# Weight rows in 2 KB packets and an fp32 down product in the expert stage of a hybrid decoder block

## The chip, the cores and the metric

The kernel runs on one core of a Trainium2 chip. The metric is the device time of one execution in microseconds (us), lower is better; the median of several runs is given, with the smallest and the largest.

## What is computed

One decoder block over N = 1024 tokens of width D = 1024, all in float32. Stick-breaking attention and a short gated convolution run side by side, are merged by sigmoid gates and projected back. Then comes the part that the change touches, a mixture of experts over 32 experts in 4 groups:

```
x  = x + merged @ w_out
h2 = rms_norm(x, norm_ffn_g)                      # (1024, 1024)
group  = top-1 of h2 @ w_rg + b_rg                # 4 groups
expert = top-2 of h2 @ w_re + b_re inside it      # 8 experts per group
for each expert e:                                # w_gate, w_up: (1024, 256); w_down: (256, 1024)
    act = silu(h @ w_gate[e]) * (h @ w_up[e]) * combine[e]
    y  += act @ w_down[e]
x  = x + y
```

Every expert's weights, 3 MB, are read once: 96 MB in all.

## The kernel before, in words

Attention, convolution, merge and their projections take the first 720 us; an `Order` class sets their order, and the change leaves them as they are. From 720 to 845 us the output projection runs over eight tiles of 128 tokens. For each tile `add_x` makes the new x in one of three buffers XR, `norm2` the norm's factor (on POOL for tiles 0 to 6, on VectorE for tile 7), `put_x` (L866) multiplies x by the norm's gain into HX and has SyncE's queue store it to the scratch tensor `h2d` and x itself to `out`, by column halves; `tr_x` and `route` compute the router's logits, and `rank` and `table` build for every expert a list `idx` of up to 88 token rows (SLOTS). The last two tiles go by column halves, in an order written out by hand.

From 845 us on the expert stage runs. For expert e, `gather` (L1093) fetches its rows from `h2d` by an indirect DMA on POOL's queue; `xT` transposes them on TensorE and splits them into a high and a low fp32r part (ScalarE's copy, VectorE's subtraction); `gateup` multiplies them with the weights in four chunks; `aT` (L1163) transposes the gated activation, `down` multiplies it with two chunks of the down weights, and ScalarE's copy (L1174) and an indirect DMA on POOL's queue that adds into `out` (L1178, the scatter) end the expert. The down product of expert e - 1 stands behind gate and up of expert e. The scatters write one tensor, so each waits until the one before has landed.

A weight chunk is [128, 1024] fp32, 512 KB. `load_chunk` (L799) loads it on SyncE's queue: a gate and up chunk holds rows i*256 + k*128 + p on partition p, so that each piece of a row that is contiguous in both places is 256 floats, 1 KB; a down chunk's are 4 KB. The chunks lie in a ring of 34 buffers (`CH`, named cha, br, chf, mg, vc, chr, x1t, hx and g after the tensors whose space they take). `split_chunk` turns a chunk into a high part (ScalarE, L1103, into WH) and a low part (VectorE, L1104, into WL), in four such buffers, three chunks ahead of TensorE; once a chunk is split, the load of the chunk 34 places on is issued. Every product with split operands is three fp32r products, `mm3`: high by high, high by low, low by high (all at L124, through `mm`).

The loop that handles experts with more than 88 tokens runs no times on this input.

Of the kernel before, what the change touches and what calls it, by code (L numbers as in the profile page):

```python
# [34 lines left out]
DE = 256  # L35
# [5 lines left out]
class Order:  # L41
    """Puts steps given in a plain sequential order into the order in which to issue them: a step
    comes once what it reads is there and what it overwrites is read, the longest chain first."""

# [54 lines left out]
def tile_hybrid_block(  # L99
# [34 lines left out]
    def warm(n):  # L134
        """Products that nothing reads, to keep the array's clock up where it would idle."""
        for _ in range(n):
            mm(PS[:, 1, :], onesB, onesB[:, None, :].to_broadcast([128, 4, 128]), True, True)

    # ------------------------------------------------------------------ constants
    wp = pool("wp")  # L140
# [60 lines left out]

    # ------------------------------------------------------------------ weights of three column blocks
    WR = {}
# [33 lines left out]

    # ------------------------------------------------------------------ first norm, transposed
    xss = xp.tile([128, 8], F32, name="xss")
# [147 lines left out]
    def unit(n, u):  # L387
# [26 lines left out]
        def scan():  # L414
            P = PT[nP]
            # a first row block's last 128 keys of a diagonal unit are all masked
            if diag:
                V.memset(bass.AP(tensor=P.tensor, offset=P.offset + w - 128, ap=[P.ap[0], [516 + 128, 2], [1, 1]]), 1.0)
            for j in range(2):
                pr = P[:, j, 0:w - 128 if diag and j == 0 else w][:, ::-1]  # L420
                V.tensor_tensor_scan(pr, pr, pr, 1.0 if diag else P[:, j, w:w + 1], op0=OP.mult, op1=OP.bypass)  # L421
            if c:
                V.tensor_copy(PT[(n + 1) % 2][:, :, 512:513], P[:, :, 0:1])
# [10 lines left out]
        for sp in range(w // 256):  # L434
            tr, x = 4 + state["sp"] % 2, state["sp"] % 3
            state["sp"] += 1
            # quarters (key block, row block); the masked one of a diagonal unit is zero
            last = diag and sp == w // 256 - 1
# [141 lines left out]

    # ------------------------------------------------------------------ transposed blocks of the other projections
    hlp = pool("hlp")
# [184 lines left out]

    # ------------------------------------------------------------------ output projection, second norm, routing
    rc = pool("rc", side="right")
# [29 lines left out]
    def load_chunk(r, i, wg, wu, wd, Y=Y):  # L799
        if i < 4:  # L800
            v = r.rearrange("p (k j c) -> p k j c", k=2, j=2)
            for j, w in enumerate((wg, wu)):
                Y.dma_start(v[:, :, j], w[i * 256:(i + 1) * 256].rearrange("(k p) c -> p k c", p=128))
        else:
            Y.dma_start(r, wd[(i - 4) * 128:(i - 3) * 128])

    def load_upto(n, ring=0, Y=Y):
        while lst["n"] < min(n, len(chunks)):
            e, i = chunks[lst["n"]]
            load_chunk(CH[lst["n"] % (ring or len(chunks))], i, w_gate_e[0, e], w_up_e[0, e], w_down_e[0, e], Y)  # L810
            lst["n"] += 1
# [54 lines left out]
    def put_x(t, half):  # L866
        tsl, hs = slice(t * 128, (t + 1) * 128), slice(half * 512, (half + 1) * 512)
        G.tensor_mul(HX[:, hs], XR[t % 3][:, hs], g2[:, hs])  # L868
        Y.dma_start(h2d[tsl, hs], HX[:, hs])
        Y.dma_start(out[tsl, hs], XR[t % 3][:, hs])  # L870
# [16 lines left out]
    def route(t):  # L887
# [26 lines left out]
        st[t] = OH, ohs, tw  # L914
        # combine weights times the norm's factor
        G.tensor_scalar(s[:, 1:2], m8[:, 0, 0:1], -1.0, None, op0=OP.mult)
# [90 lines left out]
    for t in range(2, 6):  # L1007
# [10 lines left out]
        load_upto(NCA + 11 + t - 2)  # L1018
    # the last two tiles by column halves
    for m, (half, t) in enumerate(((0, 6), (0, 7), (1, 6), (1, 7))):  # L1020
# [39 lines left out]
    table(7)  # L1060
    # slot tables
    t2 = sm.tile([128, NE], F32, name="t2")
# [3 lines left out]

    # tiles past the first of each expert, as a running count
    ext = rc.tile([128, NE], F32, name="ext")
# [13 lines left out]

    # ------------------------------------------------------------------ experts
    me = pool("me", side="right")
# [3 lines left out]
    AC = [me.tile([SLOTS, DE], F32, name="ac")] * 2  # L1088
    ACT_ = [me.tile([128, 2, 2, SLOTS], F32R, name="act")] * 2
    gate = dram.tile([1, 16], F32, name="gate")  # L1090
# [5 lines left out]

    split = {chunks[i]: HW[i] for i in range(4)}
    cst2 = {"n": 4, "h": 4}

    def split_chunk(r, key):  # L1100
        wh, wl = HW[cst2["h"] % len(HW)]
        cst2["h"] += 1
        S.activation(wh, r, AF.Copy)  # L1103
        V.tensor_sub(wl, r, wh)  # L1104
        split[key] = (wh, wl)

    def split_upto(n):
        while cst2["n"] < min(n, len(chunks)):
            e, i = chunks[cst2["n"]]
            split_chunk(CH[cst2["n"] % NC], (e, i))  # L1110
            cst2["n"] += 1
            load_upto(cst2["n"] + NC, NC)

    def expert_mm(e, i, xt, at, o):
        wh, wl = split.pop((e, i))
        if i < 4:
            for kk in range(2):
                k = 2 * i + kk
                cs = slice(kk * 512, (kk + 1) * 512)
                mm3(o, xt[0][:, k], xt[1][:, k], wh[:, cs], wl[:, cs], k == 0, k == 7)  # L1120
        else:
            k = i - 4
            for half in range(2):
                hs = slice(half * 512, (half + 1) * 512)
                mm3(PS[0:SLOTS, 2 + half, :], at[:, 0, k], at[:, 1, k], wh[:, hs], wl[:, hs], k == 0, k == 1)

# [13 lines left out]
    def gateup(e):  # L1140
        xt = XET[e % 2]
        o = PS[0:SLOTS, e % 2, :]
        sg, ac = SG[e % 2], AC[e % 2]
        for i in range(4):
            if i == 2 and e:
                aT(e - 1)
            if i == 3 and e + 1 < NE:
                xT(e + 1)
                if e + 3 < NE:
                    gather(e + 3)  # L1150
            expert_mm(e, i, xt, None, o)
            pos["n"] += 1
            if i < 3 or e < NE - 1:
                split_upto(pos["n"] + 3)
        S.activation(sg, o[:, 0:DE], AF.Silu, scale=rsl[0:SLOTS, e:e + 1])
        V.scalar_tensor_tensor(ac, o[:, DE:2 * DE], wsl[0:SLOTS, e:e + 1], sg, op0=OP.mult, op1=OP.mult)
        split_upto(pos["n"] + 3)

    def aT(e):
        ac, at = AC[e % 2], ACT_[e % 2]  # L1160
        pb = PS[:, 6, 0:2 * SLOTS].rearrange("p (k c) -> p k c", c=SLOTS)
        for k in range(2):
            T.transpose(pb[:, k], ac[:, k * 128:(k + 1) * 128], identF[0:SLOTS, 0:SLOTS])  # L1163
        S.activation(at[:, 0], pb, AF.Copy)  # L1164
        V.tensor_sub(at[:, 1], pb, at[:, 0])

    def down(e):
        at, ye = ACT_[e % 2], YE[e % 2]
        for k in range(2):
            expert_mm(e, 4 + k, None, at, None)  # L1170
            pos["n"] += 1
            split_upto(pos["n"] + 3)
        if e < NE - 1:
            S.activation(ye, PS[0:SLOTS, 2:4, :].rearrange("p b c -> p (b c)"), AF.Copy)  # L1174
        else:
            S.activation(ye[:, 0:512], PS[0:SLOTS, 2, :], AF.Copy)
            V.tensor_copy(ye[:, 512:1024], PS[0:SLOTS, 3, :])
        G.indirect_dma_start(out=out[:, :], out_offset=bass.IndirectOffsetOnAxis(ap=idx[0:SLOTS, e:e + 1], axis=0),  # L1178
                             in_=ye[:, :], in_offset=None, compute_op=OP.add)
# [3 lines left out]
    gather(1)  # L1183
    # the loads that follow stay behind the first gathers
    G.tensor_copy(AC[0][0:1, 0:1], g2[0:1, 0:1])
    for i in range(1, 4):
        early_l(i)
    load_upto(NC + 4, NC)
    xT(0)
# [9 lines left out]

    # ------------------------------------------------------------------ tokens past an expert's first slots  # L1200
    lpt = CH[6]
# [10 lines left out]
    with tc.For_i(0, nx, 1):  # L1212
# [25 lines left out]
        xT(0)  # L1238
        for i in range(6):
            split_chunk(CH[i], (-1, i))  # L1240
            expert_mm(-1, i, XET[0], ACT_[0], PS[0:SLOTS, 0, :])
            if i == 3:
                sg, ac = SG[0], AC[0]
                S.activation(sg, PS[0:SLOTS, 0, 0:DE], AF.Silu, scale=wx[0:SLOTS, 2:3])
                V.scalar_tensor_tensor(ac, PS[0:SLOTS, 0, DE:2 * DE], wx[0:SLOTS, 1:2], sg, op0=OP.mult, op1=OP.mult)
                aT(0)
        S.activation(YE[0], PS[0:SLOTS, 2:4, :].rearrange("p b c -> p (b c)"), AF.Copy)
# [32 lines left out]
```

## Time and profile before

| what | value |
|---|---|
| time, median of 3 runs (smallest, largest) | 1202.77 us (1201.70, 1204.35) |
| the profiled execution's span | 1199.3 us (the page gives no other time of its own) |
| TensorE busy | 1114.5 us, 93% |
| VectorE busy | 757.6 us, 63% |
| ScalarE busy | 644.9 us, 54% |
| POOL busy | 363.0 us, 30% |
| q1, SyncE's queue | 140360 packets, 148.12 MB, 38.2% of 16 engines' span |
| q0, POOL's indirect queue | 9216 packets, 19.95 MB, 7.7% |
| mean granted TensorE clock | 0.974 |

The page's second part cuts the span into 40 slices; the expert stage is the last 12 of them. There the DMA engines are busy nine tenths or more in nearly every slice, and hardly before. A share over the whole span therefore says little of the stage that the change touches. Busy time of POOL counts the issue of its indirect transfers; the time that they take is in the queues' rows and in the chain of waits, where a line gives start, length and what ran.

### The profile page before, as it was taken

To read this page: it belongs to the slowest core of one execution; us is meant where nothing else is said; L and a number is where in the kernel's file an instruction comes from. 1 tells how busy PE (TensorE), PEld (TensorE's weight loads), DVE (VectorE), ACT (ScalarE), POOL (GpSimd) and SP (SyncE) were. 2 spreads that over 40 slices of the span, in tenths; PEclk is the share of its full clock that TensorE was granted. 3 is DMA by queue.
4 is the path that set the end of the run, shared out by engine and by line. 5 is a ranking of instruction groups with operands and counts; after the bars stand their busy time and mean duration, and the time that the engine had idled before them with its cause. 6 is when DMAs were issued, how large, how long until landed. Compare 5 with 4: busy or idle time off the path is not lost.

```text
span 1199.3 us, 16771 instructions
## 1 busy us (share of the span) xinstructions
PE 1114.5 (93%) x5761; PEld 893.6 (75%) x5761; DVE 757.6 (63%) x1317; ACT 644.9 (54%) x1204; POOL 363.0 (30%) x658
## 2 busy tenths in 40 slices
PE   6999898999999999999999999998899999899883
PEld 5988897987888888888888887786566656566552
DVE  5579989989885332333324073445598889688772
ACT  6586767777653213222223142223588878687672
POOL 4636466463000000000000004555363334333211
PEclk9999999998999999999999999999899999899897
DMA  6000101011011111111121168928899999999993
GB/s 222 27 27 14 40 2 40 15 29 34 1 36 54 53 36 45 53 53 52 37 62 45 36 189 290 322 73 276 241 316 312 323 323 292 310 314 317 328 322 82
DMA packets 149666, 169.18 MB, mean 141 GB/s; under 512 B 14381, under 2 KB 129097, under 8 KB 149577
## 3 DMA queue, kind: packets, MB, share of 16 engines
q1 hardware_dynamic: 140360, 148.12, 38.2%
q0 software_dynamic: 9216, 19.95, 7.7%
q8 instruction: 46, 0.75, 0.2%
q14 instruction: 44, 0.35, 0.1%
HBM read 150.72 MB, written 20.45 MB: 143 GB/s over the span
## 4 chain that ended last, share of the span: by engine, by line
PE 52%; DMA 27%; DVE 8%; issue 5%; POOL 4%; ACT 2%; SPq 1%; POOLq 0%; DVEq 0%; ACTq 0%
PE PS L124 49%; DMA out_dram<-xr,idx 10%; DMA out_dram<-ye,idx 8%; DVE pt L421 3%; PE PS L446 2%; DMA cha<-in_w_down_e_dram 2%; DMA xr<-h2d,idx 1%; DMA chr<-in_w_up_e_dram 1%; DVE WL L231 1%; DVE ahl L466 1%; POOL hx L868 1%; PE PS L338 1%; DMA chr<-in_w_down_e_dram 1%; DMA mg<-in_w_down_e_dram 1%; DMA h2d<-hx 1%
## 5 line engine op out<-in xcount | busy, mean ns | idle before, releaser
L124 PE MATMUL PS<-hH,WH 128*128 128x512 f32 x448 | 143.9, 394 | 1.1 <-DVE attF L478 1.1
L124 PE MATMUL PS<-hH,WL 128*128 128x512 f32 x448 | 142.0, 390 | 0.0
L124 PE MATMUL PS<-hL,WH 128*128 128x512 f32 x448 | 141.9, 389 | 0.0
L124 PE MATMUL PS<-WH,xet 128*88 128x512 f32 x384 | 137.9, 410 | 3.5 <-ACT WH L1103 3.5
L421 DVE TENSOR_TENSOR_SCAN pt<-pt 128x128 f32<-128x128 f32 (+2 forms) x96 | 92.8, 1008 | 18.5 <-issue 13.4
L674 POOL TENSOR_TENSOR mg<-mg,sga 128x1024 f32<-128x1024 f32 x6 | 14.7, 2456 | 293.0 <-DVE sga L672 293.0
L124 PEld LDWEIGHTS PS<-hH,WL 128*128 128x128 f32 x448 | 84.1, 188 | 17.7
L124 PEld LDWEIGHTS PS<-hH,WH 128*128 128x128 f32 x448 | 84.1, 188 | 17.4 <-ACT WH L610 1.2
L124 PEld LDWEIGHTS PS<-hL,WH 128*128 128x128 f32 x448 | 84.2, 188 | 16.4
L124 PE MATMUL PS<-WH,hH 128*128 128x384 f32 x256 | 91.9, 359 | 4.4 <-ACT hH L268 2.3
L611 DVE SCALAR_TENSOR_TENSOR WL<-br,cols,WH 128x128 fp32r<-128x128 f32 x200 | 68.9, 411 | 29.3 <-ACT WH L610 29.3
L124 PE MATMUL PS<-WH,hL 128*128 128x384 f32 x256 | 87.2, 341 | 0.0
L124 PE MATMUL PS<-WL,hH 128*128 128x384 f32 x256 | 86.8, 339 | 0.0
L615 DVE TENSOR_TENSOR WL<-br,WH 128x512 fp32r<-128x512 f32 x16 | 11.1, 691 | 116.5 <-ACT WH L614 116.5
L610 ACT ACTIVATE WH<-br,cols 128x128 fp32r<-128x128 f32 x200 | 65.4, 392 | 35.6 <-PE PS L124 34.4
L124 PE MATMUL PS<-WL,xet 128*88 128x512 f32 x192 | 79.2, 413 | 4.9 <-DVE WL L1104 4.4
L124 PEld LDWEIGHTS PS<-WH,xet 128*88 128x88 f32 x384 | 61.3, 160 | 29.5 <-ACT WH L1103 4.1
L124 PE MATMUL PS<-WH,act 128*88 128x512 f32 x192 | 65.5, 395 | 1.2 <-ACT act L1164 1.2
L1178 POOL DMA_INDIRECT out_dram<-xr,idx x16 | 35.2, 2200 | 100.7 <-DMA out_dram<-ye,idx 56.0
L460 POOL CAST ahl<-zeros 128x256 fp32r<-128x256 f32 x32 | 30.4, 958 | 115.5 <-PE PS L124 107.0
L124 PE MATMUL PS<-ahl,vt 128*128 128x256 f32 x320 | 53.7, 298 | 11.4 <-DVE attF L478 10.7
L1178 POOL DMA_INDIRECT out_dram<-ye,idx x16 | 31.5, 1970 | 99.6 <-DMA out_dram<-xr,idx 75.7
(278 smaller groups left out, 2726.2 us busy)
## 6 DMA issues: line engine op xcount, KB each, us to landing
br<-in_w_in_dram SPq DMA_DIRECT2D x25, 512.0 KB
cha<-in_w_gate_e_dram SPq DMA_DIRECT2D x42, 256.0 KB
cha<-in_w_up_e_dram SPq DMA_DIRECT2D x42, 256.0 KB
cha<-in_w_down_e_dram SPq DMA_DIRECT2D x18, 512.0 KB
mg<-in_w_down_e_dram SPq DMA_DIRECT2D x17, 512.0 KB
mg<-in_w_gate_e_dram SPq DMA_DIRECT2D x29, 256.0 KB
mg<-in_w_up_e_dram SPq DMA_DIRECT2D x29, 256.0 KB
br<-in_w_in_dram SPq DMA_DIRECT2D x36, 192.0 KB
```

The costliest lines, as they stand in the source:

```text
L124: T.matmul(o, a, b, start=start, stop=stop)
L231: V.scalar_tensor_tensor(WL3[:, k], WR[idx, k // 2][:, k % 2], g1[:, k:k + 1], WH3[:, k], op0=OP.mult, op1=OP.subtract)
L338: T.transpose(pb[:, j].bitcast(F32R), st[:, a, j * 128:(j + 1) * 128], identR)
L421: V.tensor_tensor_scan(pr, pr, pr, 1.0 if diag else P[:, j, w:w + 1], op0=OP.mult, op1=OP.bypass)
L446: T.transpose(PS[:, tr, q * 128:(q + 1) * 128], BT[n % 3][:, j, (sp * 2 + sj) * 128:(sp * 2 + sj + 1) * 128], identF)
L460: G.tensor_copy(AHL[x][:, :, 0:128], zeros[:, None, :].to_broadcast([128, 2, 128]))
L466: V.tensor_sub(AHL[x][:, 1, lo:512], PS[:, tr, lo:512], AHL[x][:, 0, lo:512])
L610: S.activation(j.wH[:, k], r[:, k], AF.Copy, scale=g1[:, k:k + 1])
L611: V.scalar_tensor_tensor(j.wL[:, k], r[:, k], g1[:, k:k + 1], j.wH[:, k], op0=OP.mult, op1=OP.subtract)
L674: (G if b < 6 else V).tensor_add(mg, mg, mst[b].rearrange("p (t c) -> p t c", c=128))
L868: G.tensor_mul(HX[:, hs], XR[t % 3][:, hs], g2[:, hs])
L1178: G.indirect_dma_start(out=out[:, :], out_offset=bass.IndirectOffsetOnAxis(ap=idx[0:SLOTS, e:e + 1], axis=0), in_=ye[:, :], in_offset=None ...
```

## The change

Four things change. Gate and up chunks take their rows as p*8 + k instead of k*128 + p, so two rows lie behind one another in DRAM on each partition and a contiguous piece is 2 KB; the chunk's inside is ordered gate, then up. To match, `put_x` stores the tokens' rows with column p*8 + k at place k*128 + p: it multiplies only once both halves are there, in two POOL instructions that read every eighth element, and stores 512 KB at once. The down weights are no longer split: `down` is four fp32 products (two chunks by two column halves) straight from the loaded chunks, with an activation that isn't split either, so the two ScalarE copies and two VectorE subtractions per expert for the down chunks and VectorE's subtraction in `aT` go. And a load into a chunk's buffer is issued by `took` when that chunk has been read: a gate and up chunk after its split, a down chunk after its products. (Comments were taken out as well.)

```diff
     def load_chunk(r, i, wg, wu, wd, Y=Y):
         if i < 4:
-            v = r.rearrange("p (k j c) -> p k j c", k=2, j=2)
+            v = r.rearrange("p (j k c) -> p j k c", k=2, j=2)
             for j, w in enumerate((wg, wu)):
-                Y.dma_start(v[:, :, j], w[i * 256:(i + 1) * 256].rearrange("(k p) c -> p k c", p=128))
+                Y.dma_start(v[:, j], w.rearrange("(p k) c -> p k c", k=8)[:, 2 * i:2 * i + 2])
...
     def put_x(t, half):
         tsl, hs = slice(t * 128, (t + 1) * 128), slice(half * 512, (half + 1) * 512)
-        G.tensor_mul(HX[:, hs], XR[t % 3][:, hs], g2[:, hs])
-        Y.dma_start(h2d[tsl, hs], HX[:, hs])
+
+        if half:
+            for q in range(2):
+                c = slice(q * 512, (q + 1) * 512)
+                G.tensor_mul(HX.rearrange("t (k p) -> t k p", k=8)[:, :, q * 64:q * 64 + 64],
+                             XR[t % 3][:, c].rearrange("t (p k) -> t k p", k=8), g2[:, c].rearrange("t (p k) -> t k p", k=8))
+            Y.dma_start(h2d[tsl, :], HX)
         Y.dma_start(out[tsl, hs], XR[t % 3][:, hs])
...
-    ACT_ = [me.tile([128, 2, 2, SLOTS], F32R, name="act")] * 2
+    ACT_ = [me.tile([128, 2, SLOTS], F32, name="act")] * 2
...
+    order = [c for c in chunks if c[1] < 4]
+    place = {c: n for n, c in enumerate(chunks)}
+    read = set()
+
+    def took(c):
+
+        read.add(place[c])
+        while lst["n"] < len(chunks) and lst["n"] - NC in read:
+            load_upto(lst["n"] + 1, NC)
...
     def split_upto(n):
-        while cst2["n"] < min(n, len(chunks)):
-            e, i = chunks[cst2["n"]]
-            split_chunk(CH[cst2["n"] % NC], (e, i))
+        while cst2["n"] < min(n, len(order)):
+            c = order[cst2["n"]]
+            split_chunk(CH[place[c] % NC], c)
             cst2["n"] += 1
-            load_upto(cst2["n"] + NC, NC)
...
+            took(c)
...
+    def down_mm(e, k, r):
+        for half in range(2):
+            mm(PS[0:SLOTS, 2 + half, :], ACT_[e % 2][:, k], r[:, half * 512:(half + 1) * 512], k == 0, k == 1)
...
     def aT(e):
-        ac, at = AC[e % 2], ACT_[e % 2]
+        ac = AC[e % 2]
...
-        S.activation(at[:, 0], pb, AF.Copy)
-        V.tensor_sub(at[:, 1], pb, at[:, 0])
+        S.activation(ACT_[e % 2], pb, AF.Copy)
 
     def down(e):
-        at, ye = ACT_[e % 2], YE[e % 2]
+        ye = YE[e % 2]
         for k in range(2):
-            expert_mm(e, 4 + k, None, at, None)
-            pos["n"] += 1
-            split_upto(pos["n"] + 3)
+            down_mm(e, k, CH[place[e, 4 + k] % NC])
+            took((e, 4 + k))
```

Two places show how instructions move. On TensorE, between the transposes of the next expert's rows (identF by xr) and the next expert's gate and up products (WH, WL or hw by xet), before (`act` is the activation of the expert before):

```order
L1134 MATMUL PS<-identF,xr_5949 128x88 x8
L124 MATMUL PS<-hw_7083,xet_7082 88x512 x6
L124 MATMUL PS<-WH,act 88x512
L124 MATMUL PS<-WL,act 88x512
L124 MATMUL PS<-WH,act 88x512 x2
L124 MATMUL PS<-WL,act 88x512
L124 MATMUL PS<-WH,act 88x512 x2
L124 MATMUL PS<-WL,act 88x512
L124 MATMUL PS<-WH,act 88x512 x2
L124 MATMUL PS<-WL,act 88x512
L124 MATMUL PS<-WH,act 88x512
```

The same place after; mg, and in other experts another buffer of the ring, is the loaded chunk itself:

```order
L1146 MATMUL PS<-identF,xr_5950 128x88 x8
L124 MATMUL PS<-hw_7075,xet_7073 88x512 x6
L124 MATMUL PS<-mg,act 88x512 x4
L124 MATMUL PS<-WH,xet_7074 88x512
```

Twelve products became four, at the same place. The second place is POOL's order around the second norm of tile 6 (n2s is where its sum is made; hx from xr_5949 is tile 6, from xr_5950 tile 7; oha and ohb belong to the ranking), before:

```order
L868 TENSOR_TENSOR hx<-xr_5950,g_5954 128x512
L945 TENSOR_TENSOR oha<-oha,ohs 128x32
L946 CAST ohb<-oha 128x32
L868 TENSOR_TENSOR hx<-xr_5949,g_5954 128x512
L874 TENSOR_TENSOR n2s<-n2s 128x1
L190 TENSOR_SCALAR nrM<-n2s 128x1
```

And after:

```order
L950 TENSOR_TENSOR oha<-oha,ohs 128x32
L951 CAST ohb<-oha 128x32
L872 TENSOR_TENSOR hx<-xr_5949,g_5954 128x8x64 x2
L879 TENSOR_TENSOR n2s<-n2s 128x1
L190 TENSOR_SCALAR nrM<-n2s 128x1
```

The multiplies of the first halves of tiles 6 and 7 no longer stand earlier in the program; both of a tile now come together, tile 6's right before its norm, and tile 7's in the same way where its second half's stood, before the routing of that tile.

## Rows read from the trace of the kernel before

**Rows 1.** The page: span and the scatters' groups.

```profile
span 1199.3 us, 16771 instructions
...
L1178 POOL DMA_INDIRECT out_dram<-xr,idx x16 | 35.2, 2200 | 100.7 <-DMA out_dram<-ye,idx 56.0
...
L1178 POOL DMA_INDIRECT out_dram<-ye,idx x16 | 31.5, 1970 | 99.6 <-DMA out_dram<-xr,idx 75.7
```

**Rows 2.** Chain of waits, 930 to 1060 us: start, length, what.

```profile
936.32 8.68 DMA out_dram<-xr,idx
...
945.87 8.61 DMA out_dram<-ye,idx
...
976.81 8.38 DMA out_dram<-xr,idx
...
1028.01 9.83 DMA out_dram<-ye,idx
```

**Rows 3.** POOL timeline, 865 to 1199.3 us: start, length, instruction, [idle before].

```profile
869.52 2.30 POOL L1178 DMA_INDIRECT out_dram<-xr,idx  x1 [4.18 <-ACT xr L1174]
...
976.81 1.59 POOL L1178 DMA_INDIRECT out_dram<-xr,idx  x1 [7.42 <-DMA out_dram<-ye,idx]
...
1012.80 7.09 POOL L1178 DMA_INDIRECT out_dram<-xr,idx  x1 [4.24 <-ACT WH L1103]
...
1161.10 1.57 POOL L1178 DMA_INDIRECT out_dram<-xr,idx  x1 [11.66 <-ACT xr L1174]
...
1185.69 1.57 POOL L1178 DMA_INDIRECT out_dram<-ye,idx  x1 [6.31 <-DMA out_dram<-xr,idx]
```

**Rows 4.** TensorE (PE) timeline, 900 to 912 us.

```profile
900.11 0.32 PE L1163 MATMUL PS<-identF,ac 88*128 88x88 f32 x2
...
903.66 0.40 PE L124 MATMUL PS<-WH,act 128*88 128x512 f32 x1
...
906.47 0.39 PE L124 MATMUL PS<-WH,xet 128*88 128x512 f32 x1
...
909.23 0.32 PE L1163 MATMUL PS<-identF,ac 88*128 88x88 f32 x2
```

**Rows 5.** VectorE (DVE) timeline, 1008.5 to 1020.4 us.

```profile
1012.43 1.22 DVE L1104 TENSOR_TENSOR WL<-g,WH 128x1024 fp32r<-128x1024 f32 x1
...
1015.83 1.22 DVE L1104 TENSOR_TENSOR WL<-cha,WH 128x1024 fp32r<-128x1024 f32 x1
```

**Rows 6.** DMA, 1184 to 1192.2 us: queue, issue with median landing.

```profile
q0 software_dynamic: 144, 0.36, 31.0%
...
out_dram<-ye,idx POOLq DMA_INDIRECT x1, 6.5
```

**Rows 7.** DMA queue, 937.9 to 945.0 us: packets, MB, share.

```profile
q1 hardware_dynamic: 1752, 1.79, 72.9%
```

**Rows 8.** POOL timeline, 819 to 836 us, tile 6.

```profile
821.96 1.29 POOL L868 TENSOR_TENSOR hx<-xr,g 128x512 f32<-128x512 f32 x1 [0.68 <-DVE xr L863]
```

**Rows 9.** TensorE timeline, 825 to 840 us, router.

```profile
832.35 2.21 PE L124 MATMUL PS<-wrt,xr 128*128 128x36 f32 x16
```

**Rows 10.** VectorE groups by shape, 900 to 1160 us.

```profile
L1104 DVE TENSOR_TENSOR WL<-cha,WH 128x1024 fp32r<-128x1024 f32 x37 | 44.5, 1217 | 12.5 <-ACT WH L1103 8.4 <-ACT xr L1174 4.2
...
L1136 DVE TENSOR_TENSOR xet<-PS,xet 128x352 fp32r<-128x352 f32 x50 | 23.8, 517 | 0.1
```

**Rows 11.** DMA queue, 737 to 744 us, 2 KB stores.

```profile
q1 hardware_dynamic: 674, 1.37, 50.6%
```

**Rows 12.** DMA queue, 1029.6 to 1037.8 us.

```profile
q1 hardware_dynamic: 1500, 2.17, 80.3%
```

**Rows 13.** DMA queue, 978.4 to 985.2 us.

```profile
q1 hardware_dynamic: 1061, 1.65, 67.3%
```

**Rows 14.** DMA queues, 870 to 1167 us.

```profile
q1 hardware_dynamic: 59363, 75.79, 77.7%
q0 software_dynamic: 8076, 17.60, 27.1%
```

More of the change, by code (lines that the diff above doesn't have):

```diff
@@ L1107, in split_upto, with gateup_mm @@
     def split_upto(n):
-        while cst2["n"] < min(n, len(chunks)):
-            e, i = chunks[cst2["n"]]
-            split_chunk(CH[cst2["n"] % NC], (e, i))
+        while cst2["n"] < min(n, len(order)):
+            c = order[cst2["n"]]
+            split_chunk(CH[place[c] % NC], c)
             cst2["n"] += 1
-            load_upto(cst2["n"] + NC, NC)
[L1114 to L1125, printed above, removed]
+            took(c)
+    def gateup_mm(e, i, xt, o):
+        wh, wl = [w.rearrange("p (j k c) -> p k j c", k=2, j=2) for w in split.pop((e, i))]
+        o = o.rearrange("p (j c) -> p j c", j=2)
+        for kk in range(2):
+            k = 2 * i + kk
+            mm3(o, xt[0][:, k], xt[1][:, k], wh[:, kk], wl[:, kk], k == 0, k == 7)
+    def down_mm(e, k, r):
+        for half in range(2):
+            mm(PS[0:SLOTS, 2 + half, :], ACT_[e % 2][:, k], r[:, half * 512:(half + 1) * 512], k == 0, k == 1)
     def xT(e):
@@ L1150, in gateup @@
                     gather(e + 3)
-            expert_mm(e, i, xt, None, o)
+            gateup_mm(e, i, xt, o)
             pos["n"] += 1
@@ L1187, in tile_hybrid_block @@
         early_l(i)
-    load_upto(NC + 4, NC)
+    load_upto(NC)
+    for i in range(4):
+        took(chunks[i])
     xT(0)
@@ L1238, in tile_hybrid_block @@
         xT(0)
-        for i in range(6):
+        for i in range(4):
             split_chunk(CH[i], (-1, i))
[L1241 to L1246, printed above, removed]
+            gateup_mm(-1, i, XET[0], PS[0:SLOTS, 0, :])
+        sg, ac = SG[0], AC[0]
+        S.activation(sg, PS[0:SLOTS, 0, 0:DE], AF.Silu, scale=wx[0:SLOTS, 2:3])
+        V.scalar_tensor_tensor(ac, PS[0:SLOTS, 0, DE:2 * DE], wx[0:SLOTS, 1:2], sg, op0=OP.mult, op1=OP.mult)
+        aT(0)
+        for k in range(2):
+            down_mm(0, k, CH[4 + k])
         S.activation(YE[0], PS[0:SLOTS, 2:4, :].rearrange("p b c -> p (b c)"), AF.Copy)
```

## The prediction, made before the changed kernel had run

> **What bounds the kernel now.** I began with the page. TensorE is busy 93% of a span of 1199.3 us, which invites the reading "TensorE bound", but that share is an average, and the change touches only the last 380 us, so I read that stretch alone. The page's groups show it first: the 32 scatters of L1178 take 35.2 + 31.5 us on POOL's queue and POOL stands idle some 100 us ahead of each half of them, mostly for the landing of the other half [rows 1]. Second, the chain of waits over 930 to 1060 us: nearly every microsecond is a scatter in flight. A scatter issued at 936.32 lands 8.68 us later, and the next is issued 0.87 us after that, at 945.87 [rows 2]. They all add into `out`, so each waits for the one before. Third, POOL's timeline: from the scatter at 869.52 to that at 1185.69 lie 31 periods in 316.2 us, **10.20 us per expert** [rows 3]. TensorE needs less: between the transposes of `aT` of two experts lie 909.23 - 900.11 = 9.12 us [rows 4]. So the scatter chain sets the pace, TensorE has 1.1 us per expert to spare, and the last scatter is followed by 13.6 us that don't change.
>
> What makes a scatter slow is to be seen in two places. (a) POOL's issue of one takes 1.57 to 1.59 us when nothing disturbs it, but 7.09 us at 1012.80 [rows 3], and just then VectorE runs one 1.22 us subtraction of L1104 after another without a gap [rows 5]. (b) The landing: in a stretch with an otherwise idle queue it is 6.5 us [rows 6]; beside 1 KB weight packets 8.68 and 8.61 us [rows 2, 7].
>
> The profiled execution's span is 1199.3 us, 3.5 below the median of 1202.77; the page gives no other time of its own. I sum on the span and add 3.5.
>
> **The change, part by part.**
>
> *The head (put_x).* Before tile 6's second norm POOL had one multiply of 1.29 us (821.96) [rows 8], and one like it before tile 7's routing. Now both multiplies of a tile stand there, and they read every eighth element. If a strided one costs what the contiguous one does, that is 2 x 1.29 = 2.6 us more on the path to the first gather; if double, 1.29 x (2 x 2 - 1) x 2 = 7.7 us. The shared buffer HX is free only after a store of 512 KB instead of 256 KB, some tenths. No strided POOL multiply of this size is in the trace. I take **+4.0 us**, near the lower end, since norm and routing also wait for other engines in places. [...] The half multiplies that go from tile 6's and 7's earlier places lie in POOL's idle time: nothing.
>
> *Down product on TensorE.* Twelve products of 0.23 us go (903.66 to 906.47: 2.81 us), four fp32 products come. An fp32 product is two instructions (8 router products are x16 [rows 9]). If each costs as much per column as now, 8 x 0.234 = 1.87 us; if twice that, 16 x 0.234 = 3.74. I take 3.6, near the upper end: three fp32r products now stand for one and leave out low times low, which a full fp32 product cannot, so that four for three is the likely cost. That makes a TensorE period of 9.12 - 2.81 + 3.6 = 9.9 us. Still under 10.2, hence 0 now; but it is the floor if the scatters get faster than 9.9.
>
> *Splits that go.* Per expert VectorE loses two of six subtractions of 1.217 us, and the small one of L1165; two of 0.517 stay: 6 x 1.217 + 2 x 0.517 = 8.34 us of splits before, 5.90 after [rows 10]. A TensorE wait for a split is never last on the scatter chain, so the only gain is in (a). The 32 issues took 66.7 us [rows 1] where 32 x 1.59 = 50.9 would do: 15.8 us of excess. VectorE's load of splits falls to 0.71, and its long gapless strings, which do the harm, should fall by more. I take 0.6 of the excess: **-9.5 us**; ends -3 (gate and up chunks still come in strings) and -14.
>
> *Larger weight packets.* In a window with q1 packets of 1 KB, packet time is 72.9% x 16 engines x 7.1 us / 1752 = 47.3 ns [rows 7]; where only 2 KB packets moved, 50.6% x 16 x 7.0 / 674 = 84 ns [rows 11]. Two thirds of the weight bytes move at 84 instead of 94.6 ns per 2 KB: 11% less queue time. But loads are not what is waited for until late. What counts more: a scatter shares the engines with them. Beside mixed 1 and 4 KB packets, 80.3% x 16 x 8.2 / 1500 = 70 ns on average, a scatter landed in 9.83 us, another in such a mix (67.3% x 16 x 6.8 / 1061 = 69 ns, at 976.81) in 8.38 [rows 2, 12, 13]: 9.1 on average against 8.65 beside 1 KB alone. So 23 ns longer packets go with +0.46 us. With 2 KB packets the 1 KB stretches grow by 37 ns and the mixed ones too. Lower end: nothing, if the share goes by bytes. Upper end: in proportion to the 2.15 us above the idle landing, 2.15 x 37 / 47.3 = +1.7, and 2.3 with the mixed stretches. I take +0.5 us, the measured step, on the 28 scatters before the loads thin out: **+14 us**; ends 0 and +64 (the latter can't stand whole, see the rivals).
>
> *The end.* From 870 to 1167 us q1 takes 77.7% and q0 27.1%: the queues are full [rows 14], and the loads lose their lead. Only once does it reach the scatter chain: at 1161.10 POOL had been idle 11.66 us, against 7.42 us in a steady stretch and 6.31 at the end [rows 3], so 4.2 to 5.4 us; I take 4.6. q1's 0.777 x 297 = 231 us [rows 14], by 11% of some 70% (gate and up), makes the loads end up to 18 us sooner. This stall goes: **-4.6 us**; what is late next is the scatter again, so no more than that. Down chunks are now freed when TensorE has read them and not after their split, some three of 34 chunks less lead: hidden while the loads are ahead; once they are behind, slots stand free and no load waits for one: 0. If that cover failed it would cost a stall like the one above, up to 5 us.
>
> *Sum.* 4.0 - 9.5 + 14 - 4.6 = +3.9; 1199.3 + 3.9 + 3.5 = **1206.7 us**.
>
> **The rivals.**
> - *The landing doesn't care about packet size* (faster). For it: 8.38 us in a mix [rows 2]. Then 4.0 - 9.5 - 4.6 = -10.1; per expert 0.3 us less, 9.9, just where TensorE's floor lies, so it gets no better: about 1193 us. It decides as long as a scatter lands less than 0.2 us later than now.
> - *Landing in proportion to packet size* (much slower). For it: 8.65 at 47 ns, 9.83 at 70 ns is close to proportion. Against: 8.38. A slower chain lets the loads catch up, then the engines fall idle at times, and landings go back toward 6.5; so I halve the +2.1 us that would be left to about +1.0 per scatter: 28 + 4.0 - 9.5 - 4.6 = +17.9, 1221 us. It decides where the mean landing passes 9.6 us.
> [...]
>
> **How the numbers follow.** A measurement of this kernel tells about 0.2% (2.4 us) from no change. Forecast (1206.7) 0.38, of which a little falls below 1205.2; landing unchanged 0.30; in proportion 0.17; cancelled 0.15. Faster 0.32 (the first rival, and a little of the cancelled case with a large relief), same 0.17, slower 0.51. The range goes from 1191 (the fast rival with a head of 2.6) to 1222 (the proportional one); the forecast's own range, by the two ends of the relief, is 1202 to 1213.
>
> **What would show it.** In the profile after: mean issue of a scatter 1.7 to 1.8 us instead of 2.1; mean landing 9.5 to 10 us; period about 10.4; strided multiplies over 1.3 us each and the first gather some 4 us later; TensorE's four down products in 3.5 to 3.7 us; no idle of 11 us before a scatter near the end. Wrong if landings stay at 8.6 to 9 us and the period falls to 9.9 (fast rival), if the down products take far over 3.7 us so that TensorE becomes the pace, or if the chain runs through loads instead of scatters.

## The result and the profile after

The changed kernel takes 1208.13 us (median of 14 runs, 1204.60 to 1213.99) against 1202.44 for the kernel before in the same sessions: a ratio of 1.0054, 95% interval 1.0037 to 1.0071. It is slower by half a per cent. I had written 1206.7. The number is close; how it comes about is not what I wrote, as the runs below show.

The profiled execution after has a span of 1211.3 us, and its time on record is 1213.48 us, so it is one of the slower runs of its kernel, while the one of before stood near its median. The medians differ by 5.7 us, so about half of the 12 us between the two spans is chance. What I read from the pair is therefore checked on the kernels below, which have profiles of their own.

From the page of the changed kernel, the answer to [rows 1], with q1's row:

```profile
span 1211.3 us, 16407 instructions
...
q1 hardware_dynamic: 106440, 148.12, 37.1%
...
L1188 POOL DMA_INDIRECT out_dram<-xr,idx x16 | 27.7, 1730 | 108.3 <-DMA out_dram<-ye,idx 53.6
...
L1188 POOL DMA_INDIRECT out_dram<-ye,idx x16 | 26.8, 1675 | 104.6 <-DMA out_dram<-xr,idx 66.9
```

The scatters' issue fell from 66.7 to 54.5 us, by 12.2, as the step on the splits foresaw. q1 moves the same bytes in 106440 packets instead of 140360.

POOL's timeline after, from 815 us on, the answer to [rows 8] and [rows 3]:

```profile
825.15 2.01 POOL L872 TENSOR_TENSOR hx<-xr,g 128x512 f32<-128x512 f32 x1
...
831.49 2.02 POOL L872 TENSOR_TENSOR hx<-xr,g 128x512 f32<-128x512 f32 x1 [4.33 <-DVE xr L863]
...
841.64 4.15 POOL L872 TENSOR_TENSOR hx<-xr,g 128x512 f32<-128x512 f32 x2
...
857.68 1.31 POOL L1098 DMA_INDIRECT xr<-h2d,idx  x1 [0.85 <-issue]
...
884.01 1.63 POOL L1188 DMA_INDIRECT out_dram<-xr,idx  x1 [3.81 <-ACT xr L1184]
...
1197.80 1.57 POOL L1188 DMA_INDIRECT out_dram<-ye,idx  x1 [5.59 <-DMA out_dram<-xr,idx]
```

And the first gather of the kernel before, on the same view:

```profile
844.86 1.31 POOL L1093 DMA_INDIRECT xr<-h2d,idx  x1 [0.92 <-issue]
```

A strided multiply takes 2.01 us, not 1.29; the first gather comes 12.8 us later in this pair, not 4. (Two kernels below with the same `put_x`, e3 and e4, have it at 848.15 and 850.46 us, the ones with contiguous multiplies between 840.1 and 846.8.) From first to last scatter lie 1197.80 - 884.01 = 313.8 us, 10.12 per expert instead of 10.20: the stage behind the head is hardly faster, though its scatters are issued 12 us faster. And the stall near the end, which was to go, is still there on the same view:

```profile
1170.66 1.57 POOL L1188 DMA_INDIRECT out_dram<-xr,idx  x1 [10.30 <-ACT xr L1184]
1181.08 1.57 POOL L1188 DMA_INDIRECT out_dram<-ye,idx  x1 [8.85 <-DMA out_dram<-xr,idx]
```

TensorE's timeline after, one expert, the answer to [rows 4]:

```profile
904.83 0.32 PE L1175 MATMUL PS<-identF,ac 88*128 88x88 f32 x2
...
908.38 3.60 PE L124 MATMUL PS<-chr,act 128*88 128x512 f32 x8
...
914.59 0.32 PE L1175 MATMUL PS<-identF,ac 88*128 88x88 f32 x2
```

Four products in eight instructions, which take 3.60 us by this row, and a period of 9.76 us, by which the down product costs 9.76 - 9.12 + 2.81 = 3.45 us. I had put in 3.6.

The DMA view over 297 us of the stage after (885 to 1182 us), to be held against [rows 14], with the scatters' median landing in us:

```profile
q1 hardware_dynamic: 35288, 77.65, 76.1%
q0 software_dynamic: 8064, 17.55, 26.8%
...
out_dram<-xr,idx POOLq DMA_INDIRECT x15, 9.4
out_dram<-ye,idx POOLq DMA_INDIRECT x15, 9.2
```

The same landings before (870 to 1167 us):

```profile
out_dram<-xr,idx POOLq DMA_INDIRECT x15, 9.3
out_dram<-ye,idx POOLq DMA_INDIRECT x14, 8.5
```

Scatters land a little later, and the weights move 77.65 instead of 75.79 MB in an equally long window: 2.5% more, far from 11%. Before, 1000 bytes take 0.777 x 16 x 297 us / 75.79 MB = 48.7 ns of an engine, after 46.6. The 84 ns of a 2 KB packet that I had taken [rows 11] were those of a store with nothing beside it.

The end of the chain of waits after, from 1105 us on, shows what I had not looked for:

```profile
1116.69 13.05 DMA chr<-in_w_up_e_dram
...
1129.76 11.07 DMA x1t<-in_w_up_e_dram
...
1140.85 11.46 DMA cha<-in_w_up_e_dram
...
1162.97 9.29 DMA chf<-in_w_down_e_dram
...
1172.33 9.67 DMA mg<-in_w_up_e_dram
...
1190.65 6.29 DMA out_dram<-xr,idx
```

And the same place before, where the loads stand too, though the stretch that I had read ended ahead of them:

```profile
1141.83 10.46 DMA cha<-in_w_down_e_dram
...
1152.30 7.77 DMA br<-in_w_up_e_dram
...
1160.09 6.93 DMA mg<-in_w_up_e_dram
```

The last load in the chain lands at 1182.00 after and 1167.02 before, 29 and 32 us ahead of the span's end. So I formed theory L: **the weight loads set the end**. By it they run from the moment at which the first experts free buffers until the last chunk is there, on engines that are full all the while (q1 76.1% and q0 26.8% of them in the window above), and the head delays that moment.

### The profile page after: what moved, and what is told of

Read it like the earlier page. It is cut to its first block, busy times and chain, and to the rows that moved or that the text cites. A ratio compares the mean times of both kernels' runs of the same rounds, so it can differ in the third digit from the quotient of the medians.

```text
span 1211.3 us, 16407 instructions
## 1 busy us (share of the span) xinstructions
PE 1133.4 (94%) x5633; PEld 878.8 (73%) x5633; DVE 687.2 (57%) x1221; ACT 586.4 (48%) x1140; POOL 358.2 (30%) x658
## 3 DMA queue, kind: packets, MB, share of 16 engines
q1 hardware_dynamic: 106440, 148.12, 37.1%
## 4 chain that ended last, share of the span: by engine, by line
PE 59%; DMA 20%; DVE 8%; POOL 5%; issue 4%; ACT 2%; SPq 0%; POOLq 0%; DVEq 0%; ACTq 0%
PE PS L124 56%; DMA out_dram<-xr,idx 6%; DMA out_dram<-ye,idx 5%; DVE pt L421 3%; PE PS L446 2%; DVE ahl L466 1%; DMA chr<-in_w_up_e_dram 1%; DMA chr<-in_w_gate_e_dram 1%; DVE WL L231 1%; POOL hx L872 1%; DMA cha<-in_w_up_e_dram 1%; DMA x1t<-in_w_up_e_dram 1%; DMA mg<-in_w_up_e_dram 1%; DMA x<-in_x_dram 1%; DMA chf<-in_w_down_e_dram 1%
## 5 line engine op out<-in xcount | busy, mean ns | idle before, releaser
L124 PE MATMUL PS<-WH,xet 128*88 128x512 f32 x384 | 143.5, 433 | 0.0
L124 PE MATMUL PS<-WL,xet 128*88 128x512 f32 x192 | 76.5, 398 | 0.0
L124 PE MATMUL PS<-ahl,vt 128*128 128x256 f32 x320 | 54.5, 301 | 11.1 <-DVE attF L478 10.3
L1188 POOL DMA_INDIRECT out_dram<-xr,idx x16 | 27.7, 1730 | 108.3 <-DMA out_dram<-ye,idx 53.6
L1188 POOL DMA_INDIRECT out_dram<-ye,idx x16 | 26.8, 1675 | 104.6 <-DMA out_dram<-xr,idx 66.9
L405 ACT ACTIVATE pt<-PS 128x1024 f32<-128x1024 f32 (+1 forms) x48 | 42.5, 885 | 30.8 <-PE PS L124 30.2
```

What stands on the lines that cost most here:

```text
L124: T.matmul(o, a, b, start=start, stop=stop)
L405: S.activation(PT[nP][:, :, 0:w], z, AF.Sigmoid, scale=-1.0)
```

## The experiments

Each line is timed against the kernel before on the same chip. Ratios are to the kernel before, with their 95% interval. Lines of different chips stand in the table (the kernel before has 1202.28 to 1204.69 us on them), so lines are better compared by their ratios than by their medians; the two can differ by a few us.

| kernel | median us | ratio | interval |
|---|---|---|---|
| the change | 1208.13 | 1.0054 | 1.0037 to 1.0071 |
| e1, permutation in xT instead of put_x | 1199.39 | 0.9981 | 0.9965 to 0.9996 |
| e2, fp32 down alone | 1202.64 | 1.0002 | 0.9983 to 1.0020 |
| e3, 2 KB packets and put_x alone | 1206.92 | 1.0041 | 1.0026 to 1.0056 |
| e4, the change with 1 KB packets | 1216.29 | 1.0111 | 1.0096 to 1.0127 |
| e5, the change with contiguous multiplies | 1200.27 | 0.9995 | 0.9977 to 1.0013 |
| e6, before, scatters into two tensors | 1202.81 | 1.0014 | 0.9993 to 1.0034 |
| e7, before, last three experts' loads left out | 1198.50 | 0.9955 | 0.9935 to 0.9976 |
| e8, e1 with 1 KB packets | 1205.09 | 1.0030 | 1.0002 to 1.0059 |
| e9, e6 and e7 together | 1201.63 | 0.9997 | 0.9984 to 1.0010 |
| e10, e1 with a ring of 36 chunks | 1206.66 | 1.0045 | 1.0028 to 1.0062 |
| e11, e1 with the split down product | 1198.31 | 0.9950 | 0.9932 to 0.9968 |
| e12, e6 with 28 loads left out, spread | 1179.10 | 0.9783 | 0.9764 to 0.9801 |

### The parts one by one: e1 to e4

e1 leaves `put_x` as it was and permutes in `xT`:

```diff
-            T.transpose(pb[:, k], xe[:, kk * 128:(kk + 1) * 128], ...)
+            T.transpose(pb[:, k], xe.rearrange("t (p k) -> t k p", k=8)[:, kk], ...)
```

> The change with put_x as it was before (two contiguous multiplies, two stores, no permutation) and the permutation made in xT instead: each transpose takes every eighth column of the gathered rows. Everything after the head stays as in the changed kernel. In the profiles the first gather of the changed kernel is issued at 857.68 us, that of the kernel before at 844.86. Theory H (the head is the cost, and it is three times what I put into the sum): the first gather comes back to about 845, and the time falls by some 12 us to about 1196, below the kernel before. Theory P (my prediction: larger packets make the scatters land later, the head is worth 4): only some 4 us come back, 1204. If the strided transposes cost TensorE time, its period per expert rises above the 9.76 us of the changed kernel.

1199.39 us, 8.7 less than the change; its first gather is issued at 840.13. Theory H holds, with somewhat less than the 12 us of the one profile. The strided transposes are not free. TensorE's timeline of e1, from one expert to the next:

```profile
942.02 1.02 PE L1141 MATMUL PS<-identF,xr 88*128 88x88 f32 x8
...
952.02 1.02 PE L1141 MATMUL PS<-identF,xr 88*128 88x88 f32 x8
```

And of the change:

```profile
945.41 0.77 PE L1146 MATMUL PS<-identF,xr 88*128 88x88 f32 x8
...
955.17 0.77 PE L1146 MATMUL PS<-identF,xr 88*128 88x88 f32 x8
```

The period is 10.00 us in e1 instead of 9.76. Its scatters come every 9.98 us from first to last, so there TensorE itself is about as slow as what it feeds.

e2 takes the changed kernel with `load_chunk`, `put_x` and the order inside a chunk as before.

> Only the fp32 down product (with the loads issued as chunks are read); gate and up rows in 1 KB packets and put_x as before. Theory P: only the relief of the scatters' issue is left and the late stall, no longer landing: 1202.4 - 9.5 to -14 = 1189 to 1193. Theory L (the stage's end is set by when the weight loads are through, and these move at the engines' full rate all along): fewer splits and faster scatters are worth little, 1199 to 1203. The sum of the scatters' issue should be about 55 us as in the changed kernel (54.5) and not 66.8 as before, in both.

1202.64, a ratio of 1.0002: no gain. Yet the scatters' issue is faster, as its page shows:

```profile
L1183 POOL DMA_INDIRECT out_dram<-ye,idx x16 | 30.4, 1901 | 105.9 <-ACT WH L1112 26.9
L1183 POOL DMA_INDIRECT out_dram<-xr,idx x16 | 27.1, 1692 | 112.7 <-ACT xr L1179 30.6
```

57.5 us instead of 66.7: 9.2 us of issue are gone, close to my term of -9.5, and the time does not move. That speaks for theory L and against theory P.

e3 is the kernel before with `load_chunk`, `put_x` and the order inside a chunk of the change, and three split products down.

> Only the 2 KB packets with the permuted put_x; the down chunks are split and multiplied in three fp32r products as before. Theory H: the head of the changed kernel (12.8 us later), the scatter chain at about the pace of before or a little slower: 1212 to 1218. Theory P: +4 for the head, +14 for the landings, -4.6 at the end: 1216. The two are told apart by the profile: H wants a first gather at about 857 and a mean scatter period of about 10.2 us, P a gather at about 849 and a period of 10.7.

1206.92, below both. Its first gather stands at 848.15 us, where theory P had it and not at theory H's 857, though the profiled run (1202.69) lies 4.2 us under e3's median. But the mean period from first to last scatter is 10.03, not 10.7: theory P's landings are not there.

e4 undoes the packet size alone (the products then read the chunk in its old order, not shown):

```diff
-            v = r.rearrange("p (j k c) -> p j k c", k=2, j=2)
+            v = r.rearrange("p (k j c) -> p k j c", k=2, j=2)
```

> The changed kernel with the inside of a gate and up chunk ordered as before, so that the same rows come in pieces of 1 KB: only the packet size is undone, the permuted put_x and the fp32 down product stay. Theory P: the landings fall back by 0.5 us each, 28 of them, 14 us faster than the changed kernel: 1194. Theory L: the loads move at the rate of before, 314 instead of 321 GB/s with the gathers and scatters, over some 300 us: 5 to 7 us slower than the changed kernel, 1213 to 1215. No effect of packets: 1208.

1216.29, 8.2 us **slower** than the change, where theory P wanted 14 faster. This is the run that my prediction's largest term falls by. What the larger packets did here is to move weights faster. q1 over the same 260 us (880 to 1140) in e4:

```profile
q1 hardware_dynamic: 50878, 65.23, 78.0%
```

and in the change:

```profile
q1 hardware_dynamic: 30886, 67.28, 75.6%
```

3% more weights at a smaller share of the engines' time.

### What the head is made of: e5

```diff
-                G.tensor_mul(HX.rearrange("t (k p) -> t k p", k=8)[:, :, q * 64:q * 64 + 64],
-                             XR[t % 3][:, c].rearrange("t (p k) -> t k p", k=8), ...)
+                G.tensor_mul(HX[:, c], XR[t % 3][:, c], g2[:, c])
```

> The changed kernel with its two multiplies of a tile at the same places, but contiguous: the stored columns are not permuted (that part of the computation is changed), everything else is. In the changed kernel a strided multiply takes 2.0 us, a contiguous one of before 1.28. If the stride is the head's cost: 16 x 0.72 = 11.5 us at most, the first gather back to about 846 and the time to about 1198. If the place is the cost (both multiplies and one store only when the second half is there, so that SyncE's queue waits longer): the gather stays at 850 or later and the time at 1205 or more.

1200.27, 7.9 us less than the change. POOL's timeline of e5:

```profile
833.44 2.53 POOL L872 TENSOR_TENSOR hx<-xr,g 128x512 f32<-128x512 f32 x2
...
844.33 3.73 POOL L1097 DMA_INDIRECT xr<-h2d,idx  x1 [0.85 <-DMA x1t<-in_w_up_e_dram]
```

The two multiplies stand at the same place, 2.53 us for both, and the first gather is back at 844.33. The place costs nothing that shows; the stride costs all of it. There are 16 such multiplies, not 4, and 16 x (2.01 - 1.29) = 11.5 us is the most that this can add. The delay does grow from tile to tile: from the multiplies of tile 0 to those of tile 5 POOL takes 75.7 to 79.5 us in the three kernels with strided ones (e3, e4, the change), and 68.0 to 74.2 in six with contiguous ones (before, e1, e2, e5, e8, e11).

### What sets the end: e6, e7, e9 and e12

e6 is the kernel before with

```diff
-        G.indirect_dma_start(out=out[:, :], ...
+        G.indirect_dma_start(out=(out2 if e % 2 else out)[:, :], ...
```

and nine stores of zeros into `out2`, early.

> The kernel before, with the odd experts' scatters into a second tensor of zeros (half of the expert sums are missing from the output; the bytes moved are the same): no scatter waits for its neighbour any more, only for the one two back. If the scatter chain sets the end, as my prediction had it, the experts run at TensorE's 9.12 us instead of 10.20, up to 31 x 1.08 = 33 us faster, 1170. Theory L (the weight loads set the end): the experts run ahead, use up the loads' lead sooner and then wait for loads; the time stays within 5 us of 1202.

1202.81 us, no difference, and the timeline of POOL in e6 shows why:

```profile
946.13 1.59 POOL L1181 DMA_INDIRECT out_dram<-xr,idx  x1 [3.75 <-ACT xr L1177]
955.25 1.59 POOL L1181 DMA_INDIRECT out<-ye,idx  x1 [3.76 <-ACT ye L1177]
...
1000.86 1.59 POOL L1181 DMA_INDIRECT out_dram<-xr,idx  x1 [3.76 <-ACT xr L1177]
1012.51 1.59 POOL L1181 DMA_INDIRECT out<-ye,idx  x1 [6.29 <-ACT ye L1177]
1026.32 1.59 POOL L1181 DMA_INDIRECT out_dram<-xr,idx  x1 [10.24 <-ACT xr L1177]
```

Up to 1000.86 the scatters come every 9.12 us, at TensorE's pace. Then the lead is used up, and they come at 11.65 and 13.81 us. In the kernel before, POOL's first wait of over 10 us is the one ahead of 1161.10 [rows 3], 135 us later. What is late is a load, as ScalarE's timeline of e6 shows (the profiled run, 1209.14, lies 6.3 us above e6's median):

```profile
1024.04 1.06 ACT L1106 ACTIVATE WH<-cha 128x1024 fp32r<-128x1024 f32 x1 [4.72 <-DMA cha<-in_w_up_e_dram]
```

The split waits 4.72 us for a chunk of up weights. What the experts had won, they lose to the loads.

e7 leaves out what is loaded last:

```diff
-            load_chunk(CH[...], i, ...)
+            if e < NE - 3:
+                load_chunk(CH[...], i, ...)
```

> The kernel before without the weight loads of the last three experts, 18 of 192 chunks (their results are computed from what lies in the buffers): 9.4 MB less at the 0.252 MB per us that weights move at in this stage, so the loads are through 37 us sooner. Theory L alone: the time falls by as much as the next bound allows; since the scatter chain ran without a gap to 1148 us, that bound is near: 5 to 12 us faster, 1190 to 1197. Scatter chain alone: at most the late stall of my prediction, 4.6 us, 1198.

1198.50, 4.3 us less, which is also what the scatter chain alone would give by the expectation. I had set this up badly: the three experts without loads still have to be computed after the last chunk of the others, 3 x 9.12 = 27 us, so of the 37 us at most 10 could show. In the traces the last packet of q1 ends at 1174.1 us before and at 1145.3 in e7, 29 us sooner, and these 27 us take nearly all of that. e9 carries the same fault.

> The kernel before with both earlier edits: the odd experts' scatters into a second tensor, and no weight loads for the last three experts (half of the sums missing, the last three experts computed from old data). Each edit alone was worth little: 0 and -4.3 us. If the scatter chain and the loads are two bounds that end within some 5 us of each other (theory L with a near second bound), taking both away uncovers TensorE at 9.1 to 9.8 us per expert: 15 us or more faster, 1170 to 1187. If neither is the bound, and something that all of these kernels share is, the time stays at 1198.

1201.63: no gain, against my expectation. Here q1's last packet ends at 1148.2 us, 26 us sooner than before, and the 27 us eat that up. Neither run tells the two bounds apart. e12 does it better. It leaves out loads all over the stage, beyond the first 34 chunks, and keeps the two targets:

```diff
+            if lst["n"] < 34 or i < 4 or e % 2 == 0:
-            load_chunk(CH[...], i, ...)
+                load_chunk(CH[...], i, ...)
```

> The kernel with two scatter targets (1202.8 us), without 28 loads of down chunks of odd experts, spread over the stage (their products use old data): 14.7 MB less, 58 us of loading at 0.252 MB per us. Unlike in the kernels without the last three experts' loads, nothing is left to compute after the last load. Theory L: the experts keep TensorE's 9.12 us to the end, some 30 us faster, 1170 to 1180. If loads were not what held the kernel with two targets: no change, 1203.

1179.10, 23.7 us less than e6; by the ratios (0.9783 against 1.0014) it is 2.3%, 28 us. POOL's timeline of e12:

```profile
1054.61 1.59 POOL L1182 DMA_INDIRECT out_dram<-xr,idx  x1 [3.76 <-ACT xr L1178]
...
1100.35 1.59 POOL L1182 DMA_INDIRECT out_dram<-xr,idx  x1 [11.32 <-ACT xr L1178]
...
1163.71 1.57 POOL L1182 DMA_INDIRECT out<-ye,idx  x1 [2.96 <-ACTq L1216]
```

Now the scatters keep to 9.12 us until 1054.61 instead of 1000.86, six experts longer, and the last one is issued at 1163.71, 30.2 us sooner than in e6 (1193.92), some 6 of which belong to the run of e6 that was profiled. With the scatter chain out of the way in both, only the bytes that are loaded differ: the loads were the bound in e6, theory L, and the kernel before takes the same time as e6.

The packets in the other traces fit it. In every kernel that loads everything, q1's last packet ends 23 to 26 us ahead of the span's end, whatever the experts do: at 1174.1 of 1199.3 us before, 1186.7 of 1211.3 in the change, 1165.8 of 1191.9 in e1, 1189.3 of 1214.1 in e4. Ahead of the stage q1 stands idle with a full ring, until 848.7 us before and 861.6 in the change. From that restart to its last packet lie 318 to 325 us with 2 KB packets (the change, e1, e3, e5, e11) and 325 to 333 with 1 KB (before, e2, e4, e8); e6's profiled run, with 334, and e10 with 2 KB and 331, whose experts run at 10.40 us, stand apart. The head moves the start, the packet size the length.

### Towards a faster kernel: e8, e10, e11

e8 is e1 with e4's edit.

> The kernel with the permutation in xT, its gate and up rows in the same order but in pieces of 1 KB. It differs from the fp32-down-only kernel (1202.6) in which rows a partition takes, and from the one with the permutation in xT (1199.4) in the size of the pieces alone. If the size is what counts: 1202 to 1204, as the fp32-down-only kernel. If rows at distances of 8 KB in pieces of 1 KB are slower than straight rows (what the 8 us between the changed kernel and its 1 KB variant hint at, where 3 us lie between the other two): 1207.

1205.09. Against e1 that is 5.7 us for the packet size alone, the second pair after the change and e4 (8.2). Against e2 it is 2.5 us for the other rows and the strided transposes; the intervals overlap (1.0002 to 1.0059 and 0.9983 to 1.0020), so that part stays open.

e10 gives up one split buffer for two more chunks of the ring.

> The kernel with the permutation in xT (1199.4 us), with one of the four split buffers given up for two more chunks of the ring (36 instead of 34, splits two chunks ahead instead of three). Theory L: q1 stands idle for some 5 us while the ring is full before the first expert frees a buffer; two chunks more fill 4 of them, so the loads end 3 to 4 us sooner and so does the kernel, 1195 to 1197. Against it: TensorE waits for splits, 1200 or more.

1206.66, a miss. TensorE's timeline of e10:

```profile
946.99 1.02 PE L1139 MATMUL PS<-identF,xr 88*128 88x88 f32 x8
...
957.39 1.02 PE L1139 MATMUL PS<-identF,xr 88*128 88x88 f32 x8
```

The period is 10.40 us nearly all through the stage, 0.40 over e1's, with splits only two chunks ahead, which is the likely reason (at 945.76 TensorE stands idle for 0.17 us until a low part is there); 31 x 0.40 = 12.4 us is more than two chunks can win. It did not test the ring.

e11 is e1 with the down product split as before.

> 2 KB packets with the permutation in xT and put_x as before, and the down product split in three as before (fp32 down left out). It differs from the kernel with the permutation in xT (1199.4 us) in the down product alone. There TensorE ran at its own period of 10.01 us nearly to the end; with three fp32r products it needs about 9.12 + 0.25 = 9.4. Theory L: the loads are through at the same time, 1197 to 1200. If TensorE's period is what still holds the other kernel, up to 31 x 0.6 = 19 us less, but the loads follow close behind: 1190 to 1195.

1198.31, ratio 0.9950 (0.9932 to 0.9968), the fastest kernel here that leaves nothing out: the 2 KB packets alone, without the head's price and without the fp32 product. The ratios of e1 and e11 differ by 0.3%, their intervals overlap at the edge, so the fp32 down product is worth nothing or costs up to 4 us there. That agrees with e2.

## Why the prediction was right or wrong

The time, its sign and the range were right. The sum behind it was not; its errors cancelled, and it is luck that the number came so close.

*What bounds the kernel.* "So the scatter chain sets the pace" is the step that failed. It was true of the stretch that I read, 930 to 1060 us, where each scatter is released by the one before, but breaking the chain gained nothing, since the loads stood behind it. I had the numbers for it: q1 moved 75.79 MB in 297 us [rows 14], an expert's weights are 3.15 MB, so a load of an expert took 12.3 us while the experts ran at 10.20 [rows 3]. A ring of 34 chunks is a lead of 5.7 experts; the other 26.3 need 26.3 x 12.3 = 325 us from about 845, which is 1170, and the chain's last load landed at 1167. I used these rows only for a late stall of 4.6 us, and that stall did not go: 10.30 and 8.85 us of idle POOL stand at the same place in the change. e6 (the chain broken, no gain) and e12 (loads taken out of the same kernel, 23.7 us) show it.

*Splits that go, -9.5.* The issue became faster by 12.2 us in the change and 9.2 in e2, as worked out, and e2 shows that it is worth 0: the relief shortens a chain that is not the end.

*Larger weight packets, +14.* This had the wrong sign. In the pair of profiles the landings rose by 0.1 and 0.7 us in the medians, but that is not the packets' doing: over 880 to 1140 us the medians of the two groups of scatters are 8.7 to 9.4 us in e2, e4 and e8 with 1 KB, and 8.7 to 9.4 in e1, e3 and e11 with 2 KB. What counts is the gain in the loads' rate: e4 against the change -8.2 us, e8 against e1 -5.7, e11 against the kernel before 0.5%, 6 us. In the term "The end" I had the loads 18 us sooner, from 11% per packet, and cut it to 4.6 since "what is late next is the scatter again". 18 was too large: the 11% set a store with nothing beside it [rows 11] against loads beside scatters [rows 7], where the stage moved 2.5% more weights in the same time. The 4.6 comes near what was measured, but the reason given for it was wrong.

*The head, +4.0.* Mis-sized: 7.9 us by e5, 8.7 by e1, 10.9 by e3 against e11 (the ratios 1.0041 and 0.9950, some 0.9%). I counted the multiplies of the last two tiles, while all eight tiles go one after another through POOL, and I stayed near the lower end, a stride that costs nothing. The trace has 2.01 against 1.29, a factor of 1.56.

*Down product, 0.* Right: 3.45 or 3.60 us against 3.6, a period of 9.76 under that of the stage, no change of the time in e2.

*The sum by the runs.* Head some +9, packets some -6, fp32 down 0 to +4: +3 to +7, where 0.54%, 6.5 us, were measured. The prediction's +3.9 came from 4.0 - 9.5 + 14 - 4.6.

The rivals: they speak of landings, and none took place as written. The first had the landings right, which did not go with the packet size here (medians of 8.7 to 9.4 us with either); but its 1193 us rest on the relief of the issue, which is worth nothing. The case that did take place, loads as the bound, is named only in the last line, as "if the chain runs through loads instead of scatters", and had no price.

What stays open: whether rows at a distance of 8 KB in 1 KB pieces are slower than straight ones (e8 against e2), and how much more than e12's gain there is: its scatters wait 9 to 11 us again at 1100.35 and later, so the loads may still have been the bound there. Nor does a run show what faster loads alone would give the kernel before with its chain kept: by the waits ahead of 1161.10 [rows 3] the chain would take over some 5 us further on, so both bounds lie close together there.

## What to carry to other kernels

Where loads run ahead through a ring of buffers, compare the rate at which they come with the rate at which they are used, over the whole stage, before believing the chain of waits of a stretch in the middle: a shrinking lead hides the bound until it is gone, and whatever makes the users faster only spends it sooner. A change of the layout in memory has to be paid by an engine that has time for it: here the same permutation cost 9 us as strided multiplies on POOL ahead of the stage, and 0.24 us per expert in TensorE's period as strided reads of transposes in it. And a predicted time that comes out right is no proof of its terms; undoing one part at a time showed one term of the wrong sign, one worth nothing and one of half its size.

## What was not expected of the hardware

A transpose on TensorE that reads every eighth column cost more here than one of neighbouring columns, but little: eight of them at 1.02 instead of 0.77 us, and 0.24 us per expert in the period (10.00 against 9.76 us). And doubling the packet gained little on engines that were full (77.7% for q1 and 27.1% for q0 before [rows 14]): packet by packet, from 880 to 1140 us, the traces have on average 51.7 ns for 1 KB before and 96.1 for 2 KB after, 7% less per byte; over all bytes of the queue, with the down chunks' 4 KB packets among them, it is 48.7 against 46.6 ns per 1000 bytes (4%).
